# A scratch tile for the normed activation over twelve output tiles, a first stage in a pinned order, and the closing multiplications on one engine

## The chip, the cores and the metric

The kernel runs on one core of one Trainium2 chip. The core's engines run side by side, each through its own list of instructions in order, and wait for each other on semaphores. TensorE is PE in the profile (PEld where it loads weights), VectorE is DVE, ScalarE is ACT, GpSimd is POOL, and SyncE is SP, which issues most of the DMAs. The metric is the device time of one execution in microseconds (us); lower is better.

## The reference

A trunk of two layers works on 256 tokens of 2048 channels in fp32. The first layer is RWKV-7 time mixing, the second a chunked attention with one shared K and V, and each is followed by a squared-ReLU MLP of 8192 hidden channels. Cut to its frame:

```python
for layer in range(2):
    mod = c @ w_ada[layer] + b_ada[layer]
    sh1, sc1, gt1, sh2, sc2, gt2 = split(mod, 6)
    if layer == 1:
        h_kv = rms_norm(x, g_kv) * (1 + sc_kv) + sh_kv   # sh_kv, sc_kv = c @ w_ada_kv + b_ada_kv
        k_s, v_s = h_kv @ w_k_shared, h_kv @ w_v_shared
    h = rms_norm(x, g_mix[layer]) * (1 + sc1) + sh1
    y = rwkv7_time_mix(h, ...) if layer == 0 else chunk_band_attention(h, k_s, v_s, ...)
    x = x + gt1 * y
    h = rms_norm(x, g_mlp[layer]) * (1 + sc2) + sh2
    x = x + gt2 * (relu(h @ w_up[layer]) ** 2 @ w_down[layer])
return rms_norm(x, g_final)
# time mix: xx = shift(h) - h; six mixes h + xx * mu[j]; r, k, v = three of them @ w_r, w_k, w_v;
# decay, rate and gate by small two-step products (LoRA) of the other three
```

All weights are read once: the modulation ("ada") weights are multiplied with the single vector c, all others with 256 tokens.

## The kernel before

Channels lie on the 128 partitions: an activation is 16 blocks of 128 channels by 256 tokens, and an output tile is one such block of a product's result. A tile's weights are 16 k-blocks of 128 x 128, loaded by SP in two halves of 512 KB into the ring `raw`. Each fp32 half is split into two reduced fp32 parts: ACT casts the high part (wH, L366), DVE subtracts for the low part (wL, L369). Activations are kept as such pairs too (aHL). `proj2` multiplies wH with both parts of the activation in one product of 512 columns (L400) and wL with the high part in one of 256 (L401). `proj` makes three products of 258 columns (L389 to L391).

**The change of stage.** An MLP, and the shared K, begin while the norm of their input isn't known. So the projection ahead also writes x times its gain (`scaled`, L516), and the first SCALED = 8 output tiles are multiplied from that with `proj`, two of the 258 columns carrying the shift; the result is multiplied by the norm afterwards (L895). The norm (`rstd`) is a product of the summed squares with ones (L499), a first step on DVE (L501), two activations (L503, L504) and three DVE instructions (L506 to L508). Behind every second of the eight tiles stands one `normed` group: DVE multiplies four blocks of x with the norm (L523), ACT makes eight activations of them with gain and shift (L527), and DVE subtracts the high part. The group takes a slot of the ring `raw` for its product. The tiles after SCALED read these normed blocks with `proj2`.

**The ada work.** The modulation products of all parts but the first two run on DVE: a step is one load of 512 KB and one multiply-add of 128 x 1024 (L430), 32 steps to a part, in one long sequence. `ada_tick` takes one and two steps in turn behind output tiles that are not scaled, `ada` a given number, and `ada_need` all that are missing of the named parts, at once. A step is placed after the last DVE instruction that stood before the tile (`mark`). The second output projection calls `ada` once per tile, and its `ada_need` stands just ahead of it.

**The first stage** makes, for each of 16 blocks n of channels, the normed and shifted h, the token difference xx on POOL (L671), six mixes, and the products of block n with the LoRA weights (L722, L726) and with the rows of w_v for the first eight outputs (L730 to L732). Later blocks also make parts of further outputs (L695 to L697). The first two ada parts are made by PE here, 32 products of 32 x 128 per block in two halves (L639), then small sums (L649) and the vectors; a generator steps through them some blocks ahead. Six buffers (rawa) hold their weights, four loads to a block. The norm at the start adds squares on DVE. (An fp32 product is two records in the profile.) Where nothing else is said, a list scheduler sets each engine's order when the kernel is built; `issue_after` pins a piece of work behind a named instruction.

**The end.** The last MLP's last tile adds its two sums into x in two DVE instructions (L936), the final norm follows, and x is multiplied with it in five parts on DVE and POOL (L596), each stored by its own DMA.

## Time and profile before

| what | value |
|---|---|
| median of 3 runs | 2710.89 us (2709.28 to 2712.8) |
| the profiled execution's own time | 2713.39 us |
| its span | 2711.6 us |
| PE busy | 2623.6 us, 97% |
| DVE busy | 2043.4 us, 75% |
| ACT busy | 1364.2 us, 50% |
| POOL busy | 260.8 us, 10% |
| moved by DMA | 662.71 MB, 244 GB/s |
| first stage | 0 to about 206 us |
| first MLP begins | at 779.6 us |
| shared K begins | at about 1520 us |
| second output projection | about 1878 to 1973 us |

The span runs from the first to the last record of the execution; its own time contains what lies around that. A row of a timeline has start, duration, engine, line, operation and the tiles written and read; in brackets behind it stands the idle time ahead of it and what ended that. In a row of waits stand the waiting instruction, the one that released it, the sum in us, the number of such waits and the longest.

### The profile page before, as it was taken

What the parts mean: (1) busy time and instruction counts of PE and PEld (TensorE: products, weight loads), DVE (VectorE), ACT (ScalarE), POOL (GpSimd) and SP (SyncE); (2) the same over time, 40 slices, a digit from 0 to 9 for tenths busy, and PEclk for the clock granted to TensorE, in tenths of its full rate; (3) what the DMA queues carried; (4) which work ended last, traced back from release to release, by engine and by line L of the source; (5) the groups of instructions that cost most, each with busy time, mean ns of one, the idle gap of its engine ahead of it and who ended that gap; (6) DMA issues with size and microseconds to landing.
All of it is one profiled execution on the core that took longest, in us unless ns stands there. A gap on an engine that the chain in (4) does not pass through costs nothing.

```text
span 2711.6 us, 59299 instructions
## 1 busy us (share of the span) xinstructions
PE 2623.6 (97%) x24298; PEld 2248.0 (83%) x24298; DVE 2043.4 (75%) x2965; ACT 1364.2 (50%) x2425; POOL 260.8 (10%) x400
## 2 busy tenths in 40 slices
PE   6999999999989999999999899999989999999997
PEld 5787777778879888888888798877888888888886
DVE  5568888888768888898888786899967555566554
ACT  3346555556455543355544564455465533455443
POOL 0003333433100000000000000000100000000011
PEclk9999999999989999999999899999999999999999
DMA  9876565664757999999999588978777555555553
GB/s 347 301 245 210 177 195 168 201 207 152 245 190 272 313 328 326 324 329 329 320 320 324 194 278 278 310 254 273 246 241 249 189 191 188 187 187 190 190 187 125
DMA packets 192817, 662.71 MB, mean 244 GB/s; under 512 B 21408, under 2 KB 36128, under 8 KB 192544
## 3 DMA queue, kind: packets, MB, share of 16 engines
q1 hardware_dynamic: 190480, 656.36, 70.9%
q8 instruction: 191, 3.13, 0.4%
q10 hardware_dynamic: 2064, 2.54, 0.3%
q14 instruction: 82, 0.67, 0.1%
HBM read 656.72 MB, written 2.10 MB: 243 GB/s over the span
## 4 chain that ended last, share of the span: by engine, by line
PE 82%; DVE 5%; DMA 3%; ACT 2%; issue 1%; POOL 1%; DVEq 0%; SPq 0%; POOLq 0%; ACTq 0%
PE pj L400 43%; PE pj L401 22%; DMA rawt<-w_ada 3%; PE iv L106 2%; PE pj L391 2%; PE pj L389 2%; PE pj L390 2%; PE ms L100 1%; DVE acc L430 1%; DVE wL L369 1%; PE gr L100 1%; PE o L389 1%; PE py L320 1%; PE chn L278 0%; ACT wH L366 0%
## 5 line engine op out<-in xcount | busy, mean ns | idle before, releaser
L400 PE MATMUL pj<-aHL,wH 128*128 128x512 f32 x4352 | 1565.7, 401 | 3.9 <-DVE ks L973 1.7
L366 ACT CAST wH<-raw 128x1024 fp32r<-128x1024 f32 x772 | 806.9, 1046 | 898.0 <-PE pj L400 801.4
L401 PE MATMUL pj<-aHL,wL 128*128 128x256 f32 x4352 | 1225.8, 282 | 4.5 <-DVE wL L369 4.5
L369 DVE TENSOR_TENSOR wL<-raw,wH 128x1024 fp32r<-128x1024 f32 x772 | 941.5, 1221 | 377.5 <-ACT wH L366 371.8
L400 PEld LDWEIGHTS pj<-aHL,wH 128*128 128x128 f32 x4352 | 820.9, 189 | 201.6 <-issue 12.6
L401 PEld LDWEIGHTS pj<-aHL,wL 128*128 128x128 f32 x4352 | 822.0, 189 | 9.4 <-DVE wL L369 7.3
L400 PE MATMUL pj<-hHL,wH 128*128 128x512 f32 x1024 | 358.8, 394 | 0.0
L401 PE MATMUL pj<-hHL,wL 128*128 128x256 f32 x1024 | 284.1, 277 | 0.0
L430 DVE SCALAR_TENSOR_TENSOR acc<-rawm,ct,acc 128x1024 f32<-128x1024 f32 x184 | 235.5, 1280 | 0.9
L400 PEld LDWEIGHTS pj<-hHL,wH 128*128 128x128 f32 x1024 | 192.0, 188 | 44.5
L494 POOL TENSOR_TENSOR ss<-ss,sq 128x256 f32<-128x256 f32 x56 | 53.9, 962 | 1591.8 <-ACT sq L493 1591.5
L401 PEld LDWEIGHTS pj<-hHL,wL 128*128 128x128 f32 x1024 | 192.3, 188 | 0.0
L389 PE MATMUL pj<-aHL,wH 128*128 128x258 f32 x384 | 112.6, 293 | 29.6 <-ACT wH L366 29.6
L430 DVE SCALAR_TENSOR_TENSOR acc<-rawt,ct,acc 128x1024 f32<-128x1024 f32 x81 | 104.0, 1284 | 33.9 <-DMA rawt<-w_ada 33.6
L430 DVE SCALAR_TENSOR_TENSOR acc<-raw,ct,acc 128x1024 f32<-128x1024 f32 x95 | 123.7, 1302 | 1.0 <-DMA raw<-w_ada 0.7
L391 PE MATMUL pj<-aHL,wL 128*128 128x258 f32 x384 | 111.3, 290 | 0.9 <-DVE wL L369 0.9
L390 PE MATMUL pj<-aHL,wH 128*128 128x258 f32 x384 | 112.1, 292 | 0.0
L389 PEld LDWEIGHTS pj<-aHL,wH 128*128 128x128 f32 x384 | 75.9, 198 | 31.2 <-ACT wH L366 31.1
L936 DVE SCALAR_TENSOR_TENSOR x<-pj,mod,x 128x256 f32<-128x256 f32 x128 | 62.0, 484 | 47.0 <-PE pj L401 44.7
L391 PEld LDWEIGHTS pj<-aHL,wL 128*128 128x128 f32 x384 | 76.5, 199 | 1.5 <-DVE wL L369 1.5
L390 PEld LDWEIGHTS pj<-aHL,wH 128*128 128x128 f32 x384 | 76.1, 198 | 0.0
L639 PE MATMUL m<-rawa,crep 128*32 128x128 f32 x1024 | 42.2, 293 | 14.1 <-DMA rawa<-w_ada 13.5
(258 smaller groups left out, 2956.4 us busy)
## 6 DMA issues: line engine op xcount, KB each, us to landing
raw<-w_up SPq DMA_DIRECT2D x256, 512.0 KB, 4.3
raw<-w_down SPq DMA_DIRECT2D x256, 512.0 KB, 4.1
rawm<-w_ada SPq DMA_DIRECT2D x131, 512.0 KB, 6.3
raw<-w_ada SPq DMA_DIRECT2D x102, 512.0 KB, 4.4
rawt<-w_ada SPq DMA_DIRECT2D x87, 512.0 KB, 5.0
rawa<-w_ada SPq DMA_DIRECT2D x64, 512.0 KB, 6.3
rawm<-w_ada_kv SPq DMA_DIRECT2D x64, 512.0 KB, 6.0
raw<-w_k SPq DMA_DIRECT2D x32, 512.0 KB, 4.8
```

The source lines that it names most:

```text
L100: self.b.nc.tensor.matmul(o(c)[K], lhsT(c)[K], rhs(c)[K], start=True, stop=True)
L106: self.b.nc.tensor.matmul(o[QS[K], c, :], lhsT[QS[R], c, :], rhs[QS[R], c, :], start=True, stop=True, tile_position=(H * R, H * K))
L366: nc.scalar.copy(Hf, raw)
L369: eng.tensor_tensor(out=Lf, in0=raw, in1=Hf, op=ALU.subtract)
L389: nc.tensor.matmul(ps, H[:, i, :], a(kt)[:, 0, :], start=(first and kt == 0), stop=False)
L390: nc.tensor.matmul(ps, H[:, i, :], a(kt)[:, 1, :], start=False, stop=False)
L391: ins = nc.tensor.matmul(ps, L[:, i, :], a(kt)[:, 0, :], start=False, stop=(last and kt == KT - 1))
L400: nc.tensor.matmul(ps, H[:, i, :], a(kt), start=(first and kt == 0), stop=False)
L401: ins = nc.tensor.matmul(ps[:, 0, :], L[:, i, :], a(kt)[:, 0, :], start=False, stop=(last and kt == KT - 1))
L430: nc.vector.scalar_tensor_tensor(out=acc, in0=raw, scalar=ck, in1=acc, op0=ALU.mult, op1=ALU.add)
L494: (eng or nc.gpsimd).tensor_tensor(out=self.ss, in0=self.ss, in1=sq, op=ALU.add)
L936: nc.vector.scalar_tensor_tensor(out=x, in0=ps[:, i, :], scalar=self.mods[(layer, 5)][:, n:n + 1], in1=x, op0=ALU.mult, op1=ALU.add)
```

## The change

A tile `scr` of four blocks by 256 tokens is allocated for itself, beside the rings. It takes `normed`'s product, the squares of `ss_add` and the norm's two scratch vectors, which had buffers of their own. SCALED is 12, and a `normed` group stands behind every third of these tiles. In the attention the scaled tiles behind the fourth take an ada step each, and the four groups for the queries stand at one tile of K and three of V.

In the first stage all four parts of x are loaded first, on SP; part of the constants comes later. The squares alternate between ACT and DVE and are summed by 16 products with ones. The ada work of a block is a pair of functions instead of a generator: the products of block n + 1 are written at the start of block n, its vectors between the two halves of the v products. Each piece of PE work in a block is pinned behind the one written before it (`behind`). At the end, the last tile uses `proj` into one sum, and the multiplications with the norm are four of four blocks on DVE.

```diff
 GN_EPS = 64e-5
-SCALED = 8
+SCALED = 12
 TE = T + 2
...
         else:
-            sq = self.np.tile([P, T], F32, tag="sq", bufs=2, name="sq")
+            sq = self.scr[:, n % 2, :]
             nc.scalar.activation(sq, x, AF.Square)
...
-    def rstd(self):
+    def rstd(self, ps=None):
         nc = self.nc
-        ps = self.psm()[:, :T]
-        nc.tensor.matmul(ps, self.cst("ones"), self.ss, start=True, stop=True)
-        v = self.np.tile([P, T], F32, tag="rv", bufs=1, name="rv")
+        if ps is None:
+            ps = self.psm()[:, :T]
+            nc.tensor.matmul(ps, self.cst("ones"), self.ss, start=True, stop=True)
+        v, u = (self.scr[:, i, :] for i in (2, 3))
         nc.vector.tensor_scalar(out=v, in0=ps, scalar1=1.0 / D, scalar2=RMS_EPS, op0=ALU.mult, op1=ALU.add)
...
         nc.scalar.activation(y, y, AF.Exp, scale=-0.5)
-        u = self.np.tile([P, T], F32, tag="ru", bufs=1, name="ru")
...
         ns = range(4 * g, 4 * g + 4)
-        t = self.wp.tile([P, HK * P], F32, tag="raw", bufs=self.RAW_BUFS, name="raw").rearrange("p (a b) -> p a b", a=4)
+        t = self.scr
         nc.vector.tensor_tensor(out=t, in0=self.x[:, 4 * g:4 * g + 4, :],
...
                 r = self.rstd()
-                for lo, hi, eng in ((0, 4, nc.vector), (11, 14, nc.gpsimd), (4, 8, nc.vector), (8, 11, nc.vector),
-                                    (14, KT, nc.gpsimd)):
-                    x = self.x[:, lo:hi, :]
-                    eng.tensor_tensor(out=x, in0=x, in1=r.unsqueeze(1).to_broadcast([P, hi - lo, T]), op=ALU.mult)
-                    (nc.sync if eng is nc.vector else nc.scalar).dma_start(out=d["out"][:, lo:hi, :], in_=x)
+                for lo in range(0, KT, 4):
+                    x = self.x[:, lo:lo + 4, :]
+                    nc.vector.tensor_tensor(out=x, in0=x, in1=r.unsqueeze(1).to_broadcast([P, 4, T]), op=ALU.mult)
+                    (nc.scalar if lo % 8 else nc.sync).dma_start(out=d["out"][:, lo:lo + 4, :], in_=x)
...
             pb = self.np = s3.enter_context(tc.tile_pool(name="pb", bufs=1))
+            self.scr = pb.tile([P, 4, T], F32, name="scr")
             h = ph.tile([P, KT, T + 1], F32, name="h")
             first = CST_AT["ident"][0]
+            for q in range(4):
+                nc.sync.dma_start(out=h[:, 4 * q:4 * q + 4, 1:T + 1], in_=d["x"][:, 4 * q:4 * q + 4, :])
             nc.scalar.dma_start(out=self.csts[:, :first], in_=d["cst"][:, :first])
-            for q in range(4):
-                (nc.sync if q % 2 else nc.scalar).dma_start(out=h[:, 4 * q:4 * q + 4, 1:T + 1],
-                                                            in_=d["x"][:, 4 * q:4 * q + 4, :])
             nc.scalar.dma_start(out=self.bada, in_=d["b_ada"])
             nc.scalar.dma_start(out=self.vecs, in_=d["vecs"])
-            nc.scalar.dma_start(out=self.csts[:, first:], in_=d["cst"][:, first:])
             crep = pb.tile([P, KT, 32], F32, name="crep")
...
-            def ada_blocks():
-
-                for lo in range(KT):
-                    ps = self.psm().rearrange("p (i n) -> p i n", i=4)
-                    for part in (1, 0):
-                        raws = []
-                        for a in range(KT // HK):
-                            raw = pb.tile([P, HK, P], F32, tag="rawa", bufs=6, name="rawa")
-                            nc.sync.dma_start(out=raw, in_=d["w_ada0"][lo, part, a])
-                            raws.append(raw)
...
-                        if part:
-                            yield
...
-            adab = ada_blocks()
-            self.ss_reset()
+            def ada_load(m):
+                raws = {}
+                for part in (1, 0):
+                    for a in range(KT // HK):
+                        raw = raws[part, a] = pb.tile([P, HK, P], F32, tag="rawa", bufs=6, name="rawa")
+                        nc.sync.dma_start(out=raw, in_=d["w_ada0"][m, part, a])
+                return raws
+
+            def ada_products(m):
+                raws = ada_load(m) if m else raws0
+                ps = self.psm().rearrange("p (i n) -> p i n", i=4)
+                for part in (1, 0):
...
+                t = pb.tile([P, 2, P], F32, tag="adat", bufs=1, name="adat")
+                nc.scalar.copy(t, ps[:, 0:2, :])
+                return ps[:, 2, :], t
+
+            def ada_vectors(m, sums):
+                ps, t = sums
...
+            raws0 = ada_load(0)
+            pss = pp.tile([P, 2, T], F32, tag="t", bufs=1, name="t")[:, 0, :]
             for n in range(KT):
-                self.ss_add(h[:, n, 1:T + 1], n, nc.vector)
-            adab_at = 2
-            for i in range(adab_at):
-                next(adab)
-            r = self.rstd()
+                sq, x = self.scr[:, n % 4, :], h[:, n, 1:T + 1]
+                if n % 2:
+                    nc.vector.tensor_tensor(out=sq, in0=x, in1=x, op=ALU.mult)
+                else:
+                    nc.scalar.activation(sq, x, AF.Square)
+                nc.tensor.matmul(pss, self.cst("ones"), sq, start=(n == 0), stop=(n == KT - 1))
+            ada_vectors(0, ada_products(0))
+            r = self.rstd(pss)
...
                 xx = ph.tile([P, T], F32, tag="xx", bufs=2, name="xx")
-                nc.gpsimd.tensor_tensor(out=xx, in0=h[:, n, 0:T], in1=h[:, n, 1:T + 1], op=ALU.subtract)
+                (nc.gpsimd if n > 1 else nc.vector).tensor_tensor(out=xx, in0=h[:, n, 0:T], in1=h[:, n, 1:T + 1],
+                                                                  op=ALU.subtract)
                 return xx
+
+            def behind():
+                return tc.issue_after(self.last_pe())
...
                 raw = self.raw(d["w_v_rows"][n])
-                while adab_at < min(2 * KT, 2 * n + 4):
-                    next(adab)
-                    adab_at += 1
+                if n == 1:
+                    nc.sync.dma_start(out=self.csts[:, first:], in_=d["cst"][:, first:])
+                if n + 1 < KT:
+                    with behind():
+                        sums = ada_products(n + 1)
...
+                with behind():
...
+                for half in range(2):
+                    with behind():
+                        for i in range(4 * half, 4 * half + 4):
...
+                    if half == 0 and n + 1 < KT:
+                        with behind():
+                            ada_vectors(n + 1, sums)
                 if n == 3:
...
                 if n >= 4:
-                    v_part(n // 4 - 1, n % 4)
+                    with behind():
+                        v_part(n // 4 - 1, n % 4)
...
                 if scaled:
-                    if f % 2 == 0:
-                        self.normed(full, f // 2, rstd, up_gain, self.mods[up_sh])
+                    if f % 3 == 0:
+                        self.normed(full, f // 3, rstd, up_gain, self.mods[up_sh])
                 else:
...
                 ps = pp.tile([P, 2, T], F32, tag="pj", bufs=3, name="pj")
+                end = q == NQ - 1 and n == KT - 1
                 for b in range(FT // KT):
...
                         w = d["w_down"][layer, (q * FT // KT + b) * KT + n][:, half * HK * P:(half + 1) * HK * P]
-                        self.proj2(ps, [self.halves(self.raw(w))] * 2, lambda kt: hid[b * KT + kt],
-                                   (half * HK, half * HK + HK), b == 0, b == FT // KT - 1)
+                        mul, o = (self.proj, ps[:, 0, :]) if end else (self.proj2, ps)
+                        mul(o, [self.halves(self.raw(w))] * 2, lambda kt: hid[b * KT + kt],
+                            (half * HK, half * HK + HK), b == 0, b == FT // KT - 1)
                     self.ada_tick(layer)
                 x = self.x[:, n, :]
-                for i in range(2):
+                for i in range(2 - end):
                     nc.vector.scalar_tensor_tensor(out=x, in0=ps[:, i, :], scalar=self.mods[(layer, 5)][:, n:n + 1],
...
                 nc.scalar.activation(ks[:, j, :], ks[:, j, :], AF.Identity, bias=b)
-                if j % 2 == 0:
-                    self.normed(full, j // 2, rstd, self.gains["g_kv"], self.mods[("kv", 0)])
-                if j >= SCALED // 2:
+                if j % 3 == 0:
+                    self.normed(full, j // 3, rstd, self.gains["g_kv"], self.mods[("kv", 0)])
+                if j >= SCALED // 3:
                     self.ada(1)
...
                 project(d["w_k_shared"][j], full, ks[:, j, :], 1)
-                if j in (10, 13):
-                    self.normed(hq, (j - 10) // 3, rstd, gain, self.mods[(1, 0)])
+                if j == KT - 1:
+                    self.normed(hq, 0, rstd, gain, self.mods[(1, 0)])
...
             project(d["w_v_shared"][j], full, t, 1 + j % 2, (none, none, none, turn))
-            if j in (0, 4):
-                self.normed(hq, 2 + j // 4, rstd, gain, self.mods[(1, 0)])
+            if j in (2, 5, 8):
+                self.normed(hq, (j + 1) // 3, rstd, gain, self.mods[(1, 0)])
             turn = lambda j=j, t=t: token_major(j, t)
```

How this moves the instructions is shown at three places. The first is ACT at the start of the first MLP, around the norm's two activations, before (scr, t and hHL are scratch, the hidden tile and its pair):

```order
L516 ACTIVATE aHL<-x,gain_g_mlp_11650 128x256
L493 ACTIVATE sq<-x 128x256
L503 ACTIVATE rstd<-rv 128x256
L504 ACTIVATE rstd<-rstd 128x256
L527 ACTIVATE aHL<-raw,mod_3_73,gain_g_mlp_11650 128x256
L909 ACTIVATE hHL<-t 128x256
L527 ACTIVATE raw<-raw,mod_3_73,gain_g_mlp_11650 128x256
L910 ACTIVATE t<-t 128x256
L527 ACTIVATE aHL<-raw,mod_3_73,gain_g_mlp_11650 128x256 x2
L527 ACTIVATE raw<-raw,mod_3_73,gain_g_mlp_11650 128x256 x2
L527 ACTIVATE aHL<-raw,mod_3_73,gain_g_mlp_11650 128x256
L366 CAST wH<-raw 128x1024
```

and now:

```order
L366 CAST wH<-raw 128x1024 x2
L516 ACTIVATE aHL<-x,gain_g_mlp_11618 128x256
L493 ACTIVATE scr<-x 128x256
L366 CAST wH<-raw 128x1024 x2
L504 ACTIVATE rstd<-scr 128x256
L505 ACTIVATE rstd<-rstd 128x256
L366 CAST wH<-raw 128x1024
L527 ACTIVATE aHL<-scr,mod_3_73,gain_g_mlp_11618 128x256
L926 ACTIVATE hHL<-t 128x256
```

Before, no cast stood between the last scaled block of the projection (L516) and the end of the first normed group but the one ahead of its eighth activation; now two stand ahead of the norm's activations (L504 and L505 there) and one between them and the group.

The second is PE in the first stage, in one of its early blocks before (v, l and m are the sums of values, LoRA and ada work):

```order
L726 MATMUL l_233<-mix,lw_964 128x256
L639 MATMUL m<-rawa,crep 32x128 x8
L726 MATMUL l_233<-mix,lw_964 128x256
L731 MATMUL v_228<-aHL,wH 128x256
L732 MATMUL v_228<-aHL,wL 128x256
L639 MATMUL m<-rawa,crep 32x128 x8
L731 MATMUL v_229<-aHL,wH 128x256
L732 MATMUL v_229<-aHL,wL 128x256
L730 MATMUL v_229<-aHL,wH 128x256
L731 MATMUL v_229<-aHL,wH 128x256
```

and at the start of a block now:

```order
L705 MATMUL t<-aHL,wL 128x256
L640 MATMUL m<-rawa,crep 32x128 x32
L733 MATMUL l_213<-mix,lw_799 96x256 x2
L737 MATMUL l_214<-mix,lw_799 128x256 x2
L743 MATMUL v_209<-aHL,wH 128x256
L744 MATMUL v_209<-aHL,wH 128x256
L745 MATMUL v_209<-aHL,wL 128x256
```

The ada products stood in pieces between products of other kinds; now the 32 of a block are one run, with the LoRA's products behind it and the values' behind these.

The third is DVE in the second output projection, where L430 is an ada step and L865 (now L882) a residual addition, before:

```order
L865 SCALAR_TENSOR_TENSOR x<-pj,mod_2_78,x 128x256
L430 SCALAR_TENSOR_TENSOR acc<-rawt,ct,acc 128x1024
L865 SCALAR_TENSOR_TENSOR x<-pj,mod_2_78,x 128x256
L369 TENSOR_TENSOR wL<-raw,wH 128x1024
L517 SCALAR_TENSOR_TENSOR aHL<-x,gain_g_mlp_23613,aHL 128x256
L430 SCALAR_TENSOR_TENSOR acc<-rawt,ct,acc 128x1024
L865 SCALAR_TENSOR_TENSOR x<-pj,mod_2_78,x 128x256
L369 TENSOR_TENSOR wL<-raw,wH 128x1024
L865 SCALAR_TENSOR_TENSOR x<-pj,mod_2_78,x 128x256
L430 SCALAR_TENSOR_TENSOR acc<-rawt,ct,acc 128x1024
L369 TENSOR_TENSOR wL<-raw,wH 128x1024
L517 SCALAR_TENSOR_TENSOR aHL<-x,gain_g_mlp_23613,aHL 128x256
```

and now:

```order
L430 SCALAR_TENSOR_TENSOR acc<-rawt,ct,acc 128x1024
L882 SCALAR_TENSOR_TENSOR x<-pj,mod_2_78,x 128x256
L430 SCALAR_TENSOR_TENSOR acc<-rawt,ct,acc 128x1024
L882 SCALAR_TENSOR_TENSOR x<-pj,mod_2_78,x 128x256
L369 TENSOR_TENSOR wL<-raw,wH 128x1024
L517 SCALAR_TENSOR_TENSOR aHL<-x,gain_g_mlp_23698,aHL 128x256
L882 SCALAR_TENSOR_TENSOR x<-pj,mod_2_78,x 128x256
L369 TENSOR_TENSOR wL<-raw,wH 128x1024
L430 SCALAR_TENSOR_TENSOR acc<-rawt,ct,acc 128x1024
L882 SCALAR_TENSOR_TENSOR x<-pj,mod_2_78,x 128x256
L430 SCALAR_TENSOR_TENSOR acc<-rawt,ct,acc 128x1024
L517 SCALAR_TENSOR_TENSOR aHL<-x,gain_g_mlp_23698,aHL 128x256
```

Before, three or four other instructions stood between two ada steps; now there are pairs of steps with one instruction between them.

More of the change, by code (lines that the diff above doesn't have):

```diff
@@ new lines, in ada_products @@
+            def ada_products(m):
+                raws = ada_load(m) if m else raws0
+                ps = self.psm().rearrange("p (i n) -> p i n", i=4)
+                for part in (1, 0):
+                    for kt in range(KT):
+                        g = 32 * (kt % 4)
+                        nc.tensor.matmul(ps[g:g + 32, part, :], crep[:, kt, :], raws[part, kt // HK][:, kt % HK, :],
+                                         start=(part == 1 and kt < 4), stop=(part == 0 and kt >= KT - 4),
+                                         tile_position=(0, g))
+                t = pb.tile([P, 2, P], F32, tag="adat", bufs=1, name="adat")
+                nc.scalar.copy(t, ps[:, 0:2, :])
+                return ps[:, 2, :], t
@@ new lines, in ada_vectors @@
+            def ada_vectors(m, sums):
+                ps, t = sums
+                for part in range(2):
+                    for g in range(0, P, 32):
+                        nc.tensor.matmul(ps[g:g + 32, part:part + 1], t[:, part, g:g + 32], self.col(C_32ND),
+                                         start=True, stop=True, tile_position=(0, g))
+                o = slice(m, m + 1)
+                for part in (1, 0):
+                    bias = self.ada_src(0, part)[1]
+                    nc.vector.tensor_tensor(out=self.mods[(0, part)][:, o], in0=ps[:, part:part + 1],
+                                            in1=bias[:, o], op=ALU.add)
+                nc.vector.scalar_tensor_tensor(out=gain[:, o], in0=self.mods[(0, 1)][:, o], scalar=1.0,
+                                               in1=self.vec("g_mix0")[:, o], op0=ALU.add, op1=ALU.mult)
```

44 lines of the change are left out of this document (12 added, 32 removed).

## The prediction

> **What bounds the kernel now.** I read the page first: TensorE (PE) is busy in nearly every slice.
>
> ```profile
> span 2711.6 us, 59299 instructions
> PE   6999999999989999999999899999989999999997
> PE 82%; DVE 5%; DMA 3%; ACT 2%; issue 1%; POOL 1%; DVEq 0%; SPq 0%; POOLq 0%; ACTq 0%
> ```
>
> PE carries 82% of the chain, so a change is worth what it takes out of PE's holes or off PE's own work. The holes are at the start, at the end, and in three slices in between. Next I read the busy times by stretch at the start of the first MLP, and then the list of waits.
>
> ```profile
> 786.00:795.50 9.50, 0.00 (x0) 0.00 (x0) 5.08 (x9) 5.95 (x13) 0.00 (x0) 0.64 0.00 0
> 795.50:800.00 4.50, 4.01 (x17) 3.71 (x18) 4.49 (x4) 4.50 (x8) 0.00 (x0) 0.50 0.47 130
> 800.00:805.00 5.00, 5.00 (x35) 5.00 (x35) 2.32 (x3) 3.07 (x6) 0.00 (x0) 0.77 0.83 242
> PE pj L389 <- ACT wH L366: 29.6, 4, 9.6
> ```
>
> The columns after the stretch and its length are the busy time of PE, PEld, DVE, ACT and POOL, then PE's granted clock, DMA's share and GB/s. PE has no work for over 9 us, and behind that the granted clock is 0.50 and then 0.77. Waits of this kind, for a weight cast on ScalarE (ACT), are 29.6 us in all: one such hole at each of three places, the starts of the first MLP, of the attention and of the second MLP. The timelines of PE, ACT and DVE show what the cast waited for.
>
> ```profile
> 774.00 0.39 PE L400 MATMUL pj<-aHL,wH 128*128 128x512 f32 x1
> 779.61 0.28 PE L389 MATMUL pj<-aHL,wH 128*128 128x258 f32 x1
> 785.36 0.60 PE L499 MATMUL m<-ss,csts 128*128 128x256 f32 x2
> 795.53 0.58 PE L389 MATMUL pj<-aHL,wH 128*128 128x258 f32 x1 [9.57 <-ACT wH L366]
> 796.79 0.58 PE L391 MATMUL pj<-aHL,wL 128*128 128x258 f32 x1 [0.46 <-DVE wL L369]
> 786.46 0.42 ACT L503 ACTIVATE rstd<-rv 128x256 f32<-128x256 f32 x1 [4.79 <-DVE rv L501]
> 789.07 1.22 DVE L523 TENSOR_TENSOR raw<-x,rstd 128x1024 f32<-128x1024 f32 x1
> 790.88 0.40 ACT L909 ACTIVATE hHL<-t 128x256 fp32r<-128x256 f32 x1
> 792.97 1.08 ACT L527 ACTIVATE raw<-raw,mod,gain_g_mlp 128x256 f32<-128x256 f32 x2
> 794.45 1.03 ACT L366 CAST wH<-raw 128x1024 fp32r<-128x1024 f32 x1
> ```
>
> The first scaled tile ends at 785.4. The next tile's weights are cast at 794.45, behind the whole norm (L503) and seven of the eight activations of the first normed group (L527) in ACT's queue. So PE pays for the serial chain.
>
> **The change, part by part.**
>
> *Scratch of its own, twelve scaled tiles.* The normed group no longer takes a slot of the weight ring, and in the new order three more casts stand ahead of the norm and one right behind it. They cover the second tile and the third, so PE has two tiles, 11.5 us, to work on while the norm runs. What goes away is the idle of 29.6 us, of which 9.57, 9.39 and 9.57 are the three first waits and 1.09 the attention's second one, and twice the 0.46 for a subtraction,
>
> ```profile
> 1535.96 0.58 PE L389 MATMUL pj<-aHL,wH 128*128 128x258 f32 x1 [9.39 <-ACT wH L366]
> 1981.08 0.58 PE L389 MATMUL pj<-aHL,wH 128*128 128x258 f32 x1 [9.57 <-ACT wH L366]
> 1982.34 0.58 PE L391 MATMUL pj<-aHL,wL 128*128 128x258 f32 x1 [0.46 <-DVE wL L369]
> ```
>
> 30.5 us together, and the half clock behind it. In the first MLP that is 4.5 x 0.50 + 5 x 0.23 = 3.4 us, less what of it lies in the wait of 0.46, 3.2. The other two I take a little lower, since the same wait is 0.2 us shorter in one: 8.8 together. Total **39.3 us**.
>
> What is late next: counted from the first tile's start (779.61), DVE's product of x and the norm (L523) ends at 10.7 before, and at about 11 with a cast between the norm's steps. Eight activations (two take 1.08) and four squares of hidden tiles (L909 and its like, 0.40) on ACT run to 16.9, and the fourth tile's first cast (1.03) to 17.9. PE is through with three tiles at 3 x 5.75 = 17.25. So 0.7 us is left, and I take 1 in each place. Bounds are 0 and 5 (norm and activations 4 us later): I take **-3 us** for the three.
>
> The price is in PE's own work: a scaled tile takes three multiplications per k of 258 columns, 785.36 - 779.61 = 5.75 us, where the other kind took 779.61 - 774.00 = 5.61. Four more tiles in three stages make 12 x 0.14 = **-1.7 us**.
>
> *Ada steps pushed later.* Four tiles of the first MLP lose their ada ticks, six steps in all (1.5 a tick). Nothing hurries them until the attention's end, where all parts that the next MLP needs are finished in one go. There DVE is nearly full:
>
> ```profile
> sum 95.00, PE 88.74 PEld 76.38 DVE 83.58 ACT 43.56 POOL 14.52; mean PE 17.75 PEld 15.28 DVE 16.72 ACT 8.71 POOL 2.90
> L430 DVE SCALAR_TENSOR_TENSOR acc<-rawt,ct,acc 128x1024 f32<-128x1024 f32 x18 | 23.5, 1304 | 4.5 <-DMA rawt<-w_ada 4.4
> DVE rv L501 <- PE m L499: 4.6, 1, 4.6
> ```
>
> That is the second output projection (1878 to 1973 us). Six more steps of 1.3 us make 7.8 us of DVE. DVE's idle time there is 11.4 us, of which 4.6 is the wait at the end and 4.4 is waits on the very loads that grow in number. So 2 to 3 us can be absorbed. What queues behind an ada step on DVE are the subtractions for the weights (L369) and the residual additions that free PE's sums. Bounds 0 and -10; I take **-5 us**.
>
> *First stage.* Two limits hold here, DMA up to the fifth block, and PE from there on.
>
> ```profile
> GB/s 0 126 350 387 392 386 369 385 373 400 401 407 415 407 405 403 404 388 254 382 389 395 393 158 5 96 287 227 366 399 415 391 369 405 417 415 401 418 391 410
> 69.65 0.92 POOL L671 TENSOR_TENSOR xx<-h 128x256 f32<-128x256 f32 x1 [10.39 <-ACT h L715]
> 183.46 0.92 POOL L671 TENSOR_TENSOR xx<-h 128x256 f32<-128x256 f32 x1 [10.50 <-ACT h L715]
> 60.00:180.00 120.00, 116.70 (x1424) 92.84 (x1425) 71.08 (x154) 38.38 (x66) 9.19 (x10) 1.00 0.86 305
> h<-x ACTq DMA_DIRECT2D x2, 512.0 KB, 10.0
> ```
>
> The first row has slices of 1.5 us: DMA runs at about 390 GB/s, and falls nearly idle at 35 us, when all buffers wait on a late PE. The token difference xx marks the blocks: number 5 at 69.65, number 15 at 183.46, so 11.38 us per block. Half of x stood behind constants in ACT's queue and took 10.0 us to land; now all four parts go first on SP's. The first norm comes from 16 products with ones as x lands, and the weights' blocks follow without a hole. Up to ada block 5 the loads are x 2.1, six ada blocks 12.6, constants 0.8, first LoRA and value weights 3.8, and one later value part 0.5: 19.8 MB, at 390 GB/s from 2 us on at 53 us. The block's own 6 us of products, vectors and gain put xx of number 5 at 59 to 60.5, against 69.65: 9 to 11 us ahead. The 16 added products (one such, L499, is two records of 0.60 us together) take some 10 us as x lands and lie in the time in which PE waits for weights anyway.
>
> From there PE sets the pace. With its pieces in one run each they take:
>
> ```profile
> 36.71 1.95 PE L639 MATMUL m<-rawa,crep 128*32 128x128 f32 x64
> 38.59 1.10 PE L722 MATMUL l<-mix,lw 128*96 128x256 f32 x4
> 39.63 0.31 PE L649 MATMUL m<-csts,adat 128*32 128x1 f32 x16
> 39.87 1.13 PE L726 MATMUL l<-mix,lw 128*128 128x256 f32 x4
> 40.65 0.47 PE L730 MATMUL v<-aHL,wH 128*128 128x256 f32 x1
> 43.74 1.52 PE L639 MATMUL m<-rawa,crep 128*32 128x128 f32 x48
> ```
>
> From start to start 1.88, 1.04, 0.24, 0.78 and 3.09 us, and for the 24 products of a later value part as much as for the 24 of the block's own, 3.09: 10.1 us. DMA needs 3.375 MB / 0.39 = 8.7 us for a block. I take 10.3, since nothing fills a gap in a pinned order: ten blocks x 1.08 = 11. With the start that is 20 to 22; I take **+20 us**, bounds 10 (half the pace, a slow start) and 25.
>
> The Trainium skill, "DMA: Bandwidth & Descriptors", section "Where 436 GB/s comes from", says that for transfers out of HBM the HBM side binds at about 358 GB/s. The slices of up to 418 contradict it here; by that figure the 19.8 MB would land 4.5 us later, and the sum would be 2665.
>
> *Tail.* The last tile is summed in one piece, and the final multiplications go to DVE:
>
> ```profile
> 2702.16 1.23 DVE x L596
> 2703.38 2.74 DVEq L1141
> 2706.12 1.93 DVE x L596
> out<-x SPq DMA_DIRECT2D x2, 512.0 KB, 2.9
> out<-x SPq DMA_DIRECT2D x1, 384.0 KB, 2.5
> ```
>
> DVE stands 2.74 us while POOL runs its share, and ends at 2708.05. Four multiplications of 1.22 (L523 has the same shape) on DVE alone, from 2702.16, end at 2707.0, 1.0 earlier; the last store is 512 instead of 384 KB, 0.4 us more. The residual addition that the last tile saves makes up for it: **+1 us**, bounds 0 and 2.
>
> Sum: 39.3 - 3 - 1.7 - 5 + 20 + 1 = 50.6 us. The profiled execution took 2713.4 us (its span is 2711.6), 2.5 above the median of 2710.9: so 2662.8 by its own time, and **2660** as a median.
>
> **Rivals.**
>
> *The stall moves to the fourth tile.* The group's eight activations still form one block on ACT, and three casts wait behind it. If the norm slips by 4 us (its first step stands behind a cast that waits for PE), 5 us of idle come back in each place, and with them the clock drop of 3: 24 instead of 3, so 2681. For it: ACT is strictly in order there. Against it: before, no other hole follows the first one, though every second tile had such a block. "TensorE: Matmul & The Clock Gate" of the Trainium skill, section "What's actually happening", has the clock fall to half after about 3.4 us of idle; by that a remnant of 1 us would cost only itself, and the trace agrees so far as idles of over 9 us end at 0.50.
>
> *The first stage keeps its pace.* The last two ada loads of a block get their buffers only when half of the previous product is done. If each block then waits for them at the front of PE's order, it stays at 11.4 us and only the start is gained: 9 instead of 20, so 2671. Against it: they have 9 us to land, and such a load took 6.9.
>
> ```profile
> rawa<-w_ada SPq DMA_DIRECT2D x26, 512.0 KB, 6.9
> ```
>
> *Slower.* The same wait at full price: all of a block's 3.375 MB at the stage's 305 GB/s (11.1 us) plus a landing of 6.9, one after the other, is 18 us a block. Then 11 blocks cost 6.6 each, 73 us, no first-stage gain remains, and the time is 2711 - 31 + 73 = 2753. It decides from a block of 15 us on (11 x 3.6 = the other 31 plus 9 of the start). Against it: two of six ada buffers are always a block ahead.
>
> *Nothing gained from the scratch.* It is a single buffer; if the group's multiplication waited for an earlier reader, casts would again queue behind it, and only stage one and the tail remain: 2710.9 - 20 - 1 + 6.7 = 2697. Against it: three tiles, 17 us, lie between two groups.
>
> **How the numbers follow.** Forecast (2646 to 2670): 0.72. Stall moved (2670 to 2686): 0.12. First stage keeps its pace: 0.10. Nothing from the scratch: 0.03. Slower: 0.03. A measurement of this kernel can tell 0.2%, 5 us, from no change; all but the last give faster by far more, so faster 0.96, same 0.01, slower 0.03. Best ends: 39.3 - 1.7 + 25 + 2 = 64.6, so 2646. The poor end takes in the second and third case, 2686, and leaves out under 2 in 10. Range **2646 to 2686**.
>
> **What would show it.** At the first tile after each projection: PE idle under 2 us, clock 1.00 throughout. In the first stage: xx of block 5 near 60 and of block 15 near 163, 10.3 us apart. In the second output projection: some 25 instead of 18 ada steps, and some 5 us more between its first multiplication and the norm. At the end: four DVE multiplications without a pause. Wrong would be a wait of 5 us at the fourth tile, blocks above 11 us, or an output projection that loses over 10 us.

## The result and the profile after

The changed kernel takes **2664.7 us** (median; 2661.96 to 2667.37 in 4 runs) against 2710.97 us before: 0.9829 of the time, with a 95% interval of 0.9812 to 0.9846. That is 46 us less; the forecast was 2660 us, 51 less, in a range of 2646 to 2686. Every piece landed within 2 us of its forecast, two of them by errors that cancel.

Of the page of the changed kernel, the span, PE's busy tenths and the chain:

```profile
span 2663.8 us, 59856 instructions
PE   7999999999999999999999999999999999999998
PE 85%; DVE 6%; DMA 3%; ACT 2%; issue 2%; POOL 1%; DVEq 0%; SPq 0%; POOLq 0%; ACTq 0%
```

The eights inside PE's row are gone. The first activation of each norm (L503 before, L504 now) stands at the same place of the program in both kernels, and cuts the two profiled executions into the same pieces:

| piece, ending with | before, us | after, us | gain | forecast |
|---|---|---|---|---|
| norm of the first MLP (from the start) | 786.46 | 767.01 | 19.5 | 20 |
| norm of the attention | 740.61 | 729.13 | 11.5 | 11.7 |
| norm of the second MLP | 444.94 | 440.15 | 4.8 | 6.7 |
| last norm | 727.88 | 716.46 | 11.4 | 11.3 |
| the end | 11.71 | 11.05 | 0.7 | 1 |
| sum | 2711.6 | 2663.8 | 47.8 | 50.6 |

(The forecasts are the terms of the prediction put to these pieces: a stall with its clock loss, less 1 us for the fourth tile and 4 x 0.14 us, in the third line also less 5 us for the ada steps.)

**The transition.** The busy times by stretch after the first scaled tile of the first MLP, in the columns of the prediction (stretch, length, PE, PEld, DVE, ACT, POOL, granted clock, DMA share, GB/s), and the only wait of PE there:

```profile
766.00:775.50 9.50, 9.50 (x80) 9.44 (x79) 6.83 (x12) 7.13 (x14) 0.00 (x0) 1.00 0.49 162
775.50:780.00 4.50, 3.78 (x31) 3.57 (x31) 3.77 (x5) 3.84 (x6) 0.00 (x0) 1.00 0.05 16
780.00:785.00 5.00, 5.00 (x44) 5.00 (x43) 4.59 (x7) 4.05 (x8) 0.00 (x0) 1.00 0.69 238
778.98 0.39 PE L391 MATMUL pj<-aHL,wL 128*128 128x258 f32 x1 [0.72 <-DVE wL L369]
```

PE is full through the 9.5 us in which it stood, the clock is 1.00, and what is left is 0.72 us at the fourth tile, as forecast (1 us). PE waits there for DVE's subtraction and not for the cast: the fourth tile's first cast begins at 776.41, PE begins the tile at 777.86, and the subtraction runs from 777.71 to 778.93. The timeline of ACT shows why PE has work until then:

```profile
760.29 1.05 ACT L366 CAST wH<-raw 128x1024 fp32r<-128x1024 f32 x1 [1.77 <-PE pj L400]
763.14 1.05 ACT L366 CAST wH<-raw 128x1024 fp32r<-128x1024 f32 x1 [0.92 <-ACT scr L493]
766.04 1.05 ACT L366 CAST wH<-raw 128x1024 fp32r<-128x1024 f32 x1 [1.85 <-PE pj L390]
767.01 0.42 ACT L504 ACTIVATE rstd<-scr 128x256 f32<-128x256 f32 x1
769.28 1.05 ACT L366 CAST wH<-raw 128x1024 fp32r<-128x1024 f32 x1 [1.41 <-PE pj L390]
772.84 1.08 ACT L527 ACTIVATE aHL<-scr,mod,gain_g_mlp 128x256 fp32r<-128x256 f32 x2
776.41 2.93 ACT L366 CAST wH<-raw 128x1024 fp32r<-128x1024 f32 x3
```

The three casts at 760.29, 763.14 and 766.04 stand ahead of the norm (L504), where before there were none between the first tile's and the norm; one stands between the norm and the group (L527), and then come three together. The first four are the casts of the second and the third tile: PE has two tiles to work on while the norm and the group run.

**The first stage.** Its blocks, by the token difference xx of number 5 and of number 15, and its busy times over the stretch that the prediction showed:

```profile
65.74 0.61 POOL L675 TENSOR_TENSOR xx<-h 128x256 f32<-128x256 f32 x1 [6.83 <-ACT h L725]
164.65 0.61 POOL L675 TENSOR_TENSOR xx<-h 128x256 f32<-128x256 f32 x1 [9.33 <-ACT h L725]
60.00:180.00 120.00, 119.81 (x1528) 110.49 (x1529) 82.27 (x172) 53.31 (x85) 6.75 (x11) 1.00 0.85 319
```

A block takes 9.89 us where it took 11.38; the forecast was 10.3. But number 5 comes at 65.7, 3.9 us ahead of before, and not 9 to 11. The start lost what the pace won: 3.9 + 14.9 = 18.8 at number 15, where 20 to 22 were forecast. What holds the start is in SP's timeline and in the wait lists of SP and PE:

```profile
17.39 2.52 SPq L631 DMA_DIRECT2D rawa<-w_ada  x3
29.14 0.33 SPq L718 DMA_DIRECT2D csts<-cst  x1
SPq L718 <- PE m L651: 9.1, 1, 9.1
35.76 0.65 PE L640 MATMUL m<-rawa,crep 128*32 128x128 f32 x16 [3.60 <-DMA rawa<-w_ada]
```

The second load of constants stands in SP's queue and waits 9.1 us for a small product (L651) that reads the constants. That product reads columns of the first load only, so the wait must come from the tile of constants being tracked as one. All later loads stand behind it, and at 35.76 PE has waited 3.60 us for one of them.

**The second output projection.** The busy times of a stretch of the same length as in the prediction, up to the norm, and the group of ada steps in it:

```profile
1841.00:1936.00 95.00, 85.90 (x607) 73.83 (x606) 87.23 (x103) 41.76 (x60) 11.94 (x14) 0.98 0.86 292
L430 DVE SCALAR_TENSOR_TENSOR acc<-rawt,ct,acc 128x1024 f32<-128x1024 f32 x22 | 29.0, 1317 | 4.8 <-DMA rawt<-w_ada 4.8
PE pj L401 <- DVE wL L369: 7.2, 6, 2.4
```

PE does 2.8 us less in the same time, DVE 3.7 more, and PE waits 7.2 us for subtractions (3.2 before). Four of the six ada steps put off stand in this stretch (22 of L430 against 18); the forecast had some 25. DVE's waits on the ada loads are 4.8 us, where they were 4.4. What the steps cost in all is measured below.

**The end.** The four multiplications run without a pause:

```profile
2655.03 4.63 DVE L596 TENSOR_TENSOR x<-x,rstd 128x1024 f32<-128x1024 f32 x4
```

### The profile page after: what moved, and what is told of

Read it like the earlier page. It is cut to its first block, busy times and chain, and to the rows that moved or that the text cites. A ratio compares the mean times of both kernels' runs of the same rounds, so it can differ in the third digit from the quotient of the medians.

```text
span 2663.8 us, 59856 instructions
## 1 busy us (share of the span) xinstructions
PE 2612.3 (98%) x24584; PEld 2264.6 (85%) x24584; DVE 2041.0 (77%) x2959; ACT 1358.0 (51%) x2413; POOL 248.7 (9%) x396
## 4 chain that ended last, share of the span: by engine, by line
PE 85%; DVE 6%; DMA 3%; ACT 2%; issue 2%; POOL 1%; DVEq 0%; SPq 0%; POOLq 0%; ACTq 0%
PE pj L400 42%; PE pj L401 21%; PE pj L390 2%; PE pj L389 2%; PE pj L391 2%; DMA rawt<-w_ada 2%; PE iv L106 2%; DVE wL L369 2%; DVE acc L430 2%; PE ms L100 1%; PE gr L100 1%; PE m L640 1%; PE o L389 1%; PE t L704 1%; PE t L705 1%
## 5 line engine op out<-in xcount | busy, mean ns | idle before, releaser
L400 PE MATMUL pj<-aHL,wH 128*128 128x512 f32 x4128 | 1489.6, 402 | 2.8 <-DVE x L882 2.8
L401 PE MATMUL pj<-aHL,wL 128*128 128x256 f32 x4128 | 1164.3, 282 | 7.8 <-DVE wL L369 7.6
L400 PEld LDWEIGHTS pj<-aHL,wH 128*128 128x128 f32 x4128 | 780.3, 189 | 190.6 <-issue 12.7
L400 PE MATMUL pj<-hHL,wH 128*128 128x512 f32 x992 | 347.4, 394 | 0.0
L401 PE MATMUL pj<-hHL,wL 128*128 128x256 f32 x992 | 275.2, 277 | 0.0
L430 DVE SCALAR_TENSOR_TENSOR acc<-rawm,ct,acc 128x1024 f32<-128x1024 f32 x178 | 228.0, 1281 | 0.7
L494 POOL TENSOR_TENSOR ss<-ss,scr 128x256 f32<-128x256 f32 x56 | 51.5, 919 | 1583.8 <-ACT scr L493 1555.8
L391 PE MATMUL pj<-aHL,wL 128*128 128x258 f32 (+1 forms) x608 | 171.1, 281 | 1.7 <-DVE wL L369 1.7
L390 PE MATMUL pj<-aHL,wH 128*128 128x258 f32 (+1 forms) x608 | 172.4, 284 | 0.0
L389 PE MATMUL pj<-aHL,wH 128*128 128x258 f32 (+1 forms) x608 | 172.1, 283 | 0.0
L430 DVE SCALAR_TENSOR_TENSOR acc<-rawt,ct,acc 128x1024 f32<-128x1024 f32 x87 | 112.1, 1289 | 25.2 <-DMA rawt<-w_ada 25.0
L430 DVE SCALAR_TENSOR_TENSOR acc<-raw,ct,acc 128x1024 f32<-128x1024 f32 x95 | 124.0, 1305 | 0.6 <-DMA raw<-w_ada 0.4
L391 PEld LDWEIGHTS pj<-aHL,wL 128*128 128x128 f32 x608 | 115.8, 191 | 2.3 <-DVE wL L369 2.3
L390 PEld LDWEIGHTS pj<-aHL,wH 128*128 128x128 f32 x608 | 115.0, 189 | 0.1
L389 PEld LDWEIGHTS pj<-aHL,wH 128*128 128x128 f32 x608 | 114.4, 188 | 0.1
L927 ACT ACTIVATE t<-t 128x256 f32<-128x256 f32 x128 | 53.4, 417 | 3.6
```

The lines of the kernel that those rows point to most:

```text
L389: nc.tensor.matmul(ps, H[:, i, :], a(kt)[:, 0, :], start=(first and kt == 0), stop=False)
L390: nc.tensor.matmul(ps, H[:, i, :], a(kt)[:, 1, :], start=False, stop=False)
L391: ins = nc.tensor.matmul(ps, L[:, i, :], a(kt)[:, 0, :], start=False, stop=(last and kt == KT - 1))
L400: nc.tensor.matmul(ps, H[:, i, :], a(kt), start=(first and kt == 0), stop=False)
L401: ins = nc.tensor.matmul(ps[:, 0, :], L[:, i, :], a(kt)[:, 0, :], start=False, stop=(last and kt == KT - 1))
L430: nc.vector.scalar_tensor_tensor(out=acc, in0=raw, scalar=ck, in1=acc, op0=ALU.mult, op1=ALU.add)
```

## The experiments

**The parts alone.** First, the transitions without the new first stage and end. This is the kernel before with

```diff
-SCALED = 8
+SCALED = 12
...
-        t = self.wp.tile([P, HK * P], F32, tag="raw", bufs=self.RAW_BUFS, name="raw").rearrange("p (a b) -> p a b", a=4)
+        t = self.scr
...
+                    if f % 3 == 0:
+                        self.normed(full, f // 3, rstd, up_gain, self.mods[up_sh])
```

and what belongs to it in the attention.

> The kernel before with only the scratch tile, twelve scaled tiles and the new places of the normed groups; first stage and end as before. Theory (the parts add up): the norms stand 11.5, 4.8 and 11.4 us closer to the one before in the changed kernel's trace, 27.7 us in all, so 2683 us, with the first stage at 11.4 us a block. Rival (a quicker first stage is needed for the transitions' gain, or the other way round): more than 6 us off, 2690 or 2676.

Measured: 2686.93 us (2683.82 to 2689.18), 0.9907 [0.9888, 0.9925] of before. Then what is left without them, the first stage and the end:

```diff
-SCALED = 12
+SCALED = 8
...
-        t = self.scr
+        t = self.wp.tile([P, HK * P], F32, tag="raw", bufs=self.RAW_BUFS, name="raw").rearrange("p (a b) -> p a b", a=4)
```

with the old places of the groups (the squares and the norm's vectors keep the scratch, here and in the next run).

> The changed kernel with eight scaled tiles, the old places of the groups and the group's slot in the weight ring: what is left is the new first stage and the new end. Theory (the parts add up): 2711 - 18.8 for the first stage - 0.7 for the end = 2691 us, with the three waits of 9.5 us. Rival (some of the first stage's gain is lost at the next transition): above 2697 us.

Measured: 2690.10 us (2686.3 to 2692.35), 0.9918 [0.9899, 0.9937]. The gains are 24.0 and 20.9 us, 44.9 together, where both at once gave 46.3. The parts add up within what can be told.

**The slot or the number.** Is it the scratch or the third tile to a group that takes the stall away? First the changed kernel with the slot back:

```diff
-        t = self.scr
+        t = self.wp.tile([P, HK * P], F32, tag="raw", bufs=self.RAW_BUFS, name="raw").rearrange("p (a b) -> p a b", a=4)
```

> The changed kernel, but the normed group takes a slot of the weight ring again; still twelve scaled tiles. Theory (the slot is what kept the casts behind the group): the waits of 9.5 us and the half clock are back in three places, 36 to 39 us, so about 2700 us. Rival (three tiles to a group are what covers the norm): the waits stay away, 2665 us.

Measured: 2704.91 us (2698.59 to 2707.39), 0.9973 [0.9963, 0.9982]. From its list of waits and the timelines of PE and ACT at the first MLP:

```profile
PE pj L389 <- ACT wH L366: 28.5, 3, 9.6
776.73 0.58 PE L389 MATMUL pj<-aHL,wH 128*128 128x258 f32 x1 [9.57 <-ACT wH L366]
767.66 0.42 ACT L504 ACTIVATE rstd<-scr 128x256 f32<-128x256 f32 x1 [4.79 <-DVE scr L502]
775.65 1.03 ACT L366 CAST wH<-raw 128x1024 fp32r<-128x1024 f32 x1
```

All three holes are back, to the hundredth of a us in the first MLP, and the cast stands behind the norm and seven activations again. Twelve tiles without the scratch take none of the stall away. Then the scratch without the twelve tiles:

```diff
-SCALED = 12
+SCALED = 8
...
-                    if f % 3 == 0:
-                        self.normed(full, f // 3, rstd, up_gain, self.mods[up_sh])
+                    if f % 2 == 0:
+                        self.normed(full, f // 2, rstd, up_gain, self.mods[up_sh])
```

with the old places of the groups in the attention.

> The changed kernel with the scratch tile, but eight scaled tiles and a normed group behind every second of them, as before; the groups for the queries stand where they stood before. Theory (the scratch alone takes the stall away): two tiles take PE 11.5 us, and ACT needs four casts, eight activations and four squares, 10.0 us, so no hole of over 2 us comes back; 1.7 us of PE work and six ada steps (7 us in the second output projection) are saved: about 2656 us. Rival (twelve are needed): the groups come late, a hole of 3 to 5 us at each of three places, 2672 us or more.

Measured: 2659.69 us (2658.87 to 2660.39), 0.9808 [0.9788, 0.9828]. PE's waits for casts are small:

```profile
PE pj L389 <- ACT wH L366: 2.4, 3, 1.1
```

So the scratch does it alone. The kernel with eight tiles is not slower than the changed one: its median is 5 us lower, though the two intervals of their ratios overlap. With the new first stage and end in all of them, the medians of the four kernels are:

| scaled tiles | group in the ring's slot, us | group in the scratch, us |
|---|---|---|
| eight | 2690.10 | 2659.69 |
| twelve | 2704.91 | 2664.70 |

The scratch is worth 30.4 us with eight tiles and 40.2 with twelve. The twelve tiles, with the new places of the groups, cost 14.8 us with the slot and 5.0 with the scratch. By the profiles, the 14.8 lie in the piece between the attention's norm and the second MLP's (440.5 against 455.3 us), where the ada steps that they put off are done.

**The steps put off.** The changed kernel with ada ticks behind the later scaled tiles too:

```diff
-                else:
+                if f >= 8 or not scaled:
                     self.ada_tick(layer)
```

> The changed kernel with ada ticks behind the scaled tiles 8 to 11 of the MLPs too, so that no ada step is pushed on. Theory (the steps pushed on cost the second output projection 7 us of waits and 2 us of half clock): 87 instead of 93 steps from the attention's ring, waits of PE in that projection back to under 6 us, time 2657 us. Rival (DVE is as full in the first MLP, where the groups are made, so that the steps hold up subtractions there): waits of 2 us and more among tiles 9 to 13, time 2664 us or more.

Measured: 2652.72 us (2649.79 to 2654.34), 0.9786 [0.9773, 0.9798], below the interval of the changed kernel. The piece between the attention's norm and the second MLP's takes 426.5 us in its profile, where the changed kernel takes 440.2; the first MLP takes as long as it did (729.2 and 729.1). PE's waits in that piece, here with the ticks:

```profile
PE pj L401 <- DVE wL L369: 3.9, 6, 1.3
PE pj L400 <- DVE x L882: 1.3, 1, 1.3
PE m L442 <- DVE acc L430: 0.2, 1, 0.2
PE pj L391 <- DVE wL L369: 0.2, 1, 0.2
```

and in the changed kernel:

```profile
PE pj L401 <- DVE wL L369: 7.6, 7, 2.4
PE pj L400 <- DVE x L882: 2.8, 2, 2.2
PE m L1022 <- DVE vf L992: 2.3, 2, 2.1
PE m L442 <- DVE acc L430: 1.3, 1, 1.3
PE pj L391 <- DVE wL L369: 0.2, 1, 0.2
```

That is 5.6 against 14.2 us, 8.6 of the 13.6. The rest is clock: three of the changed kernel's waits (at 1684, 1835 and 1892, the first well ahead of the second output projection) are followed by some 3.4 us at half clock, 1.7 us lost each time (shown in the last section), and the kernel with the ticks has none there. So six steps put off cost 13.6 us, more than twice the 5 that were forecast. Two more profiles, with and without the ticks on top of the moved constants (below), have the piece at 428.6 and 440.8 us, 12.2 apart. In the profile of the kernel with eight tiles, which puts none off but has the old places of the groups, the piece takes 432.3 us. The other 5.8 us of the 426.5 come with the twelve tiles or with the new places of the groups for the queries; which of the two wasn't separated.

**More of it.** If six steps drawn forward gain, do more? This one starts from the kernel with both edits, ticks and constants (below), and draws 7 steps more forward by the count of loads (80 instead of 87 from the attention's ring):

```diff
-                if f >= 8 or not scaled:
+                if f >= 3 or not scaled:
                     self.ada_tick(layer)
```

> The changed kernel with the constants' load ahead of any reader and ada ticks behind the scaled tiles 3 to 11 of the MLPs (before 8 to 11), 7 or 8 steps more out of the attention's share. Theory (each step put off costs the second output projection about 2 us, so each one drawn forward still gains): the 4.4 us of PE waits there go, 2645 us. Rival (DVE sets the limit: it is busy 40.0 of 44 us in the four groups' tiles, and 7.5 steps of 1.3 us are 9.8): new waits for subtractions in the first MLP's tiles 3 to 12, 2652 us or more.

Measured: 2656.12 us (2652.24 to 2658.87), 0.9794 [0.9781, 0.9808]. No gain. The output projection's waits fall, but in the list of waits this stands, in a stretch of the attention ahead of it:

```profile
PE pT L1066 <- DVE s L1055: 2.6, 1, 2.6
PE m L1021 <- DVE vf L991: 1.4, 1, 1.4
```

The piece takes 428.1 us against 428.6, while each MLP loses some 2.5 us: over the whole execution PE's waits for subtractions in `proj` (L391) rise from 1.6 to 4.0 us, in part as the rival had it. The wait has only moved.

**The constants.** The load that held up SP, moved ahead of all that reads constants:

```diff
             raws0 = ada_load(0)
+            nc.sync.dma_start(out=self.csts[:, first:], in_=d["cst"][:, first:])
...
-                if n == 1:
-                    nc.sync.dma_start(out=self.csts[:, first:], in_=d["cst"][:, first:])
```

> The changed kernel with the second load of constants (546 KB) on SP right behind the first ada block's loads, ahead of any reader, in place of behind the second block's LoRA and value loads, where SP stood 9.1 us on a matmul that reads constants. Theory (that wait runs the DMA queues dry at 27 to 31 us and starves the third block): the idle of 3.6 us ahead of the third block's ada products and the half clock behind it (1.7 us) go, token difference 5 comes at about 61 instead of 65.7, and the time is 2660 us. Rival (PE's own work sets the pace by then, or the constants, loaded earlier, cost as much): 2664 us, token difference 5 at 64 or later.

Measured: 2661.68 us (2658.87 to 2663.97), 0.9820 [0.9807, 0.9832]; 3.0 us below the changed kernel, not clear of it. The stretch that was dry, 20 to 40 us, with the edit:

```profile
20.00:40.00 20.00, 17.91 (x275) 14.60 (x268) 12.73 (x30) 5.71 (x12) 0.61 (x1) 0.83 1.03 402
```

and in the changed kernel:

```profile
20.00:40.00 20.00, 14.95 (x170) 11.39 (x171) 10.37 (x24) 4.97 (x9) 0.00 (x0) 0.76 0.87 332
```

DMA moves 402 instead of 332 GB/s there and never stops, and the token difference 5 comes at 62.2 instead of 65.7. But the clock differs between profiles too, so one is not enough. Here are those of the nine kernels of this study with the pinned order, by the granted clock between 18 and 30 us:

| load of the constants | clock, 18 to 30 us | number 5 at | number 15 at |
|---|---|---|---|
| late (changed kernel, slot back, first stage and end alone) | partly 0.50 | 65.7, 66.0, 67.1 | 164.7, 164.9, 166.0 |
| late (eight tiles, ticks) | 1.00 | 63.1, 62.8 | 162.3, 162.0 |
| ahead (this kernel, and three other kernels that keep the edit) | partly 0.50 | 62.2, 62.4, 63.9, 63.0 | 161.4, 161.3, 163.1, 161.9 |

With parts at half clock in both, the load ahead brings number 15 some 3.3 us earlier on average (161.9 for 165.2). What it brings at a full clock no profile shows. With the ticks as well:

> The changed kernel with both edits, the constants' load ahead of any reader and ada ticks behind the scaled tiles 8 to 11. If both theories hold the gains add, 5 and 8 us, to 2652 us; if only the load's does, 2660; if only the ticks' does, 2657.

Measured: 2649.68 us (2649.14 to 2652.89), 0.9778 [0.9765, 0.9790]; again 3.0 us below its counterpart, whose interval overlaps. Twice the same size and the same sign, and the 3.3 us of the profiles, speak for the load, and the dry stretch is gone in the profile; its worth of 3 us is likely and not proven. This is the fastest kernel of the study, 15 us below the changed one.

**The pinned order.** The new first stage without the ties between the pieces:

```diff
             def behind():
-                return tc.issue_after(self.last_pe())
+                return nullcontext()
```

> The changed kernel without the pinned order: the pieces of a block of the first stage are written as now, but a piece isn't tied behind the one written before it. Theory (the pinned order makes the pace): blocks of 11.4 us again from the fifth on, 15 us more, 2680 us. Rival (the new writing, with a block's ada products in one piece, makes it): blocks of 9.9 us, 2665 us.

Measured: 2692.23 us (2685.4 to 2697.71), 0.9931 [0.9917, 0.9944]. The pace is that of before, 11.45 us, and number 5 comes at 76.2, so the loss is 27.5 us and not only 15. The new writing alone makes the stage slower than before (69.7 and 11.4). The same nine blocks (number 6 to number 15), free:

```profile
87.72:190.70 102.98, 99.89 (x1221) 79.96 (x1220) 60.95 (x133) 33.67 (x58) 8.29 (x9) 1.00 0.80 287
L640 PE MATMUL m<-rawa,crep 128*32 128x128 f32 x576 | 23.2, 279 | 0.0
```

and pinned:

```profile
75.33:164.65 89.32, 89.32 (x1227) 82.34 (x1226) 61.79 (x132) 34.38 (x58) 5.53 (x10) 1.00 0.91 340
L640 PE MATMUL m<-rawa,crep 128*32 128x128 f32 x576 | 17.6, 274 | 0.0
```

The same products, at a full clock in both, keep PE busy for 99.9 us in pieces and for 89.3 in runs. The 576 ada records alone take 23.2 and 17.6 us. Waits are only the other 3.1 us. What the pinned order saves is PE's own time.

**The ones.** PE's first product waits for the 66 KB of constants with the ones, in the changed kernel's list of waits:

```profile
PE t L669 <- DMA csts<-cst: 6.3, 1, 6.3
```

Loaded ahead of x, on top of the kernel with ticks from tile 3 on:

```diff
+            nc.sync.dma_start(out=self.csts[:, :first], in_=d["cst"][:, :first])
             for q in range(4):
...
-            nc.scalar.dma_start(out=self.csts[:, :first], in_=d["cst"][:, :first])
```

> As the run with ticks behind tiles 3 to 11, and the first part of the constants (66 KB, the ones among them) loaded on SP ahead of x, since PE's first product waits 6.3 us for it while the first squares are ready at 5.5. Theory (the ones are late): the first norm comes about 0.8 us earlier, and the time falls by as much, within what can be told. Rival (loads set the pace until the fifth block): token difference 5 at the same time, no change.

Measured: 2655.13 us (2649.82 to 2659.1), 0.9787 [0.9774, 0.9801], no difference to 2656.12. The first norm stands at 15.56 us in both profiles; the product now waits for its square:

```profile
PE t L670 <- ACT scr L669: 6.2, 1, 6.2
```

## Why the prediction was right, and where it wasn't

- **The stall** (39.3 - 3 us) was right in cause. The group's slot in the weight ring kept the casts behind it: with the slot the holes return, without it they go even at eight tiles. The prediction's words, that the casts "cover the second tile and the third", are what ACT's timeline shows. In size, its 36.3 us lie between the 30.4 and the 40.2 that the scratch is worth with eight tiles and with twelve. The 0.7 us left at the fourth tile was worked out to the end of a cast and measured as 0.72; but PE waited for the subtraction behind that cast, which the working left out, so that close an agreement is luck.
- **The twelve tiles** were taken as part of that gain. The stall goes without them. With the ticks kept, they and the new places of the groups bring at most 5.8 us in the attention and 2.8 in the two MLPs, by the profiles of the two kernels; without the ticks, they cost what follows.
- **The ada steps** (-5 us) were mis-sized: six of them cost 13.6 us of the attention's piece and 12 of the median. The step that failed is "2 to 3 us can be absorbed": the six steps added 8.6 us of PE waits, more than the 7.8 us that they take on DVE, so none of it shows as absorbed, and DVE's waits on the ada loads in the projection did not shrink. The term also has no clock in it: of four new PE waits of over 2 us three were followed by half clock, 5 us together. It didn't show in the sum, since that piece gained some 7 us elsewhere that the prediction hadn't seen. Some 5 of them are in the traces: beside the hole, the kernel before has 9.3 us of other waits there, one of 1.75 us (at 1633.65) with half clock behind it, and the kernel with the ticks has 5.6 us and no half clock.
- **The first stage** (+20 us, measured 19.5) was right as a sum of two wrong parts. Its start should have gained 9 to 11 us and gained 3.9: "the weights' blocks follow without a hole" failed at SP's queue, where the moved load of constants waited 9.1 us. The diff showed that move, and the prediction left it out. The load moved ahead gives back some 3 us. The other thing left out is the clock: behind short waits for weights the mean granted clock from 18 to 30 us was 0.72, and the two kernels with the late load and a full clock there have number 5 some 3.4 us earlier (62.9 for 66.3 on average). No run is free of both, so whether the rest of the forecast for the start holds stays open. The pace was forecast at 10.3 us and is 9.9: the estimate from runs in the trace of before was good, and what the pinned order does, join PE's pieces, was the mechanism. The rival "keeps its pace" fell.
- **The end** (+1 us) measured 0.7 us in this profile.
- The rival of the stall at the fourth tile fell (PE waits 0.7, 0.2 and 0.7 us at the three places, not 5). That of nothing from the scratch fell with the same profile, as did the slower one: from 60 to 206 us, behind the fourth block, PE has no wait for a load.

## What to carry to other kernels

A buffer taken from a shared ring orders its user among the ring's other users; a scratch place of its own for a serial chain lets the work that covers the chain pass it. Work that is put off costs where it is done at last, so read there whether the engine that gets it has idle time that is not a wait on the same work. And a load moved in a queue takes its waits along: what it waits for, by the tile as it is tracked, stops everything behind it.

## What the runs showed of the hardware

**Short holes can cost the clock too.** The prediction took a remnant of 1 us to cost only itself; the remnants of 0.7 us did so, but longer waits often did not. From the waits of PE behind the first stage, in the twelve profiled executions: none of the 31 waits of 1.2 to 1.65 us (the last norm's left out) was followed by half clock, 6 of 13 from 1.7 to 2.0 us, and 9 of 12 from 2.1 to 2.6. The length of one wait doesn't decide it alone: two waits of 1.13 and 1.14 us were followed by half clock too, one of them with a second wait of 0.56 us close behind it, and in the changed kernel's first stage one of 1.30 us, at 18.88, stands ahead of some 7 us of it. One of the 9, in the changed kernel, its wait and the stretches behind it:

```profile
1684.42 0.44 PE L1022 MATMUL m<-csts,vf 128*128 128x128 f32 x2 [2.10 <-DVE vf L992]
1685.30:1688.70 3.40, 3.40 (x12) 2.86 (x11) 2.70 (x3) 1.31 (x2) 0.00 (x0) 0.51 0.88 323
1688.70:1692.00 3.30, 3.30 (x22) 2.70 (x20) 2.38 (x4) 1.05 (x1) 0.00 (x0) 1.00 0.93 325
```

Here the half clock starts 0.9 us after PE goes on and lasts 3.4 us, so a hole of 2.1 us cost 3.8. Of the 6 and 9 cases, 13 have 3.4 us of it, and two 6.8. "TensorE: Matmul & The Clock Gate" of the Trainium skill, section "HAM oscillation — how this bites in real kernels", puts the limit at idle gaps of about 3.4 us; here waits of 1.7 to 2.6 us suffice more often than not, and the measurement decides.

**PE pays for short runs.** The same products took 99.9 us in pieces and 89.3 in runs (above), at the same granted clock. A short run, in the kernel without the pinned order:

```profile
130.03 0.28 PE L743 MATMUL v<-aHL,wH 128*128 128x256 f32 x1
130.24 0.64 PE L640 MATMUL m<-rawa,crep 128*32 128x128 f32 x16
130.82 0.39 PE L744 MATMUL v<-aHL,wH 128*128 128x256 f32 x1
131.04 0.28 PE L745 MATMUL v<-aHL,wL 128*128 128x256 f32 x1
```

Inside a run the value products start 0.12 us apart. The step into the ada run takes 0.21 us, and the first step behind it 0.22. Four such runs of 16 take 4 x 0.58 = 2.32 us, where 64 records in one run take 1.89 (107.80 to 109.69 in the changed kernel). That makes 0.09 + 0.10 + 0.14 = 0.33 us for each added run. Without the pinned order a block has four ada runs instead of one, 27 more in nine blocks: by estimate 9 of the 10.6 us. The ada products differ from the value products in two ways, full fp32 and a result in groups of 32 partitions; which of the two costs the time, no run here separates.
